# Decayed running sum of a matrix product: two quarters of w trade engines, and the first piece of x is turned and used in two halves

## The chip, the cores and the metric

The kernel runs on one core of a Trainium2 chip. A core has a matrix engine (TensorE, PE in the profile, with its weight loads shown apart as PEld), three engines for element-wise work (VectorE or DVE, ScalarE or ACT, GpSimd or POOL), a queue engine (SyncE or SP) and 16 DMA engines. The metric is the time of one execution on the device in microseconds, lower is better; the median of several runs is given.

## The reference

```python
def setup_inputs():
    B, S, D = (16, 2048, 1024)
    return {'x': np.random.randn(B, S, D).astype(np.float32), 'w': np.random.randn(D, D).astype(np.float32), 'decay': (0.9 * np.random.rand(D) + 0.05).astype(np.float32)}

def reference(x, w, decay):
    xw = x @ w
    out = np.zeros_like(xw)
    out[:, 0, :] = xw[:, 0, :].copy()
    for t in range(1, S):
        out[:, t, :] = decay[None, :] * out[:, t - 1, :] + xw[:, t, :]
    return out.astype(np.float32)
```

A product of x (16 batches of 2048 steps of 1024 values) with one 1024 x 1024 matrix, and then, in each of the 1024 columns, a running sum over the steps that decays by that column's factor.

## The kernel before

**Tiling.** Time is cut into chunks of 512 steps, 64 chunks in all, and pairs of chunks of one batch form groups. The 1024 output columns are eight tiles of 128 (n = 0 to 7), and the contraction over 1024 is eight passes of 128 (k = 0 to 7). Output tiles stand with the columns on the partitions and time along the row, so that the decayed sum is one scan instruction of VectorE along the row. Each pair (group, n) is a slot: eight passes of k for each of its two chunks, 16 matmuls of 512 columns, accumulated in a PSUM tile of two banks ("ps", three of them in a ring; "spare" and "spare1" are one bank each).

**x.** A chunk is loaded by four DMAs from GpSimd's queue, one for each group of 32 partitions (`load`, L105), which turn f32 into bf16 on the way. VectorE transposes it in 32 x 32 blocks on pairs of bf16 values seen as one f32 (`turn`, L115): m names a pair of passes, k = 2m and 2m + 1, and j the block of 32 steps. ScalarE or VectorE then separates even from odd (`part`, L123), which gives "xt". A matmul may take its moving operand from xt, or straight from the transposed pairs "xw" with a stride (the argument `pairs` of `matmul`, L131).

**w.** It is loaded in four quarters (`load_w`, L319): h is the half of the columns, e tells even from odd k. Of each quarter four casts (`settle`, L326), one for each k, bring it into its place in "wsb". Number i of a cast means h = i // 8, e = i // 4 % 2, m = i % 4. So 0 to 3 are the first quarter, 4 to 7 the second, 8 to 11 the third (columns n = 4 to 7, even k) and 12 to 15 the fourth (n = 4 to 7, odd k). The first quarter comes from the queues of SyncE and ScalarE, the other three from GpSimd's.

**Slots after the product.** A paired slot has its odd steps joined with the even steps before them, so that the scan runs over half the length: ScalarE copies the PSUM tile (letter p, L191) and makes the decayed even ones (g, L171), GpSimd adds (j, L205), VectorE scans (S, L210), ScalarE and GpSimd fill in the other half (h and c, L171 and L266). An unpaired slot is scanned by VectorE from PSUM directly (S, L229); slots 1 and 3 are such, slots 0 and 2 are paired. VectorE transposes the result back (B, L278), SyncE stores it (L302). k saves the last value for the next group (L270), z prepares the first (L199, L201), d copies the squared decays (L385).

**Order.** Every instruction is pinned to the order in which it is written; each engine carries out its own in that order. The order is an agenda written out by hand, a list of two- or three-character deeds for each step (a slot number, or -99 for the opening). Capital W settles on VectorE, small w on ScalarE; E is a transpose of one m of one of the four first pieces of x, F and G are the even-odd casts of such a piece on VectorE and ScalarE; M, U and L are loads. The matmuls of slots 0 to 3 are written at step 0, ahead of the deeds of that step; those of slot s at step s.

**The opening.** Chunks 0 and 1 come in two pieces each (`cuts`: ten and six blocks of 32 steps for chunk 0, seven and nine for chunk 1). Ten passes of TensorE on zeros (five f32 matmuls, two passes each, L345) run while the first piece is on its way. `spin_on(3)` (K3) has ScalarE copy one value of the first piece's last 32 partitions into "gate", and one bf16 matmul on gate follows it. Then come the transposes, and the matmuls of slots 0 to 3, first over all eight k of the first piece (even k from xw, odd k from xt), then of the second piece, then of chunk 1. Slot 0 to 2 use the three ps tiles, slot 3 the spares. Slot 4 is the first that reads the third and fourth quarters of w, even k first and then odd k, and its PSUM tile is slot 0's.

Of the kernel before, what the change touches and what calls it, by code (L numbers as in the profile page):

```python
# [14 lines left out]
def _ap(ap_obj: bass.AP, new_ap, extra_offset=0):  # L15
    return dataclasses.replace(
        ap_obj,
        ap=[list(p) for p in new_ap],
        offset=ap_obj.offset + extra_offset,
    )  # L20
# [5 lines left out]
def kernel(  # L26
# [26 lines left out]
    nc = tc.nc  # L53
    pin = tc.keep_in_program_order
    B, S, D = x.shape
# [3 lines left out]
    P = 32  # L59
    CQ = D // NQ  # L60
    K = CQ // P
    M = K // 2
    TL = 512
    NJ = TL // P
    NC = S // TL
    R = K // 2
# [9 lines left out]
    def ring(pool, name, count, shape, dtype=FP32):  # L76
        i = turns[name] = turns.get(name, -1) + 1
        return pool.tile(shape, dtype, name=f"{name}{i % count}")

    def quad(q):  # L80
        return slice(q * P, (q + 1) * P)
# [15 lines left out]
    xb_of = {}  # L97
    xw_of = {}
    xt_of = {}
# [10 lines left out]
    def turn(c, j0=0, j1=NJ, m0=0, m1=M):  # L110
        if c not in xw_of:
            xw_of[c] = ring(sb, "xw", 2, [128, M, NJ, P, 2], BF16)
        src = xb_of[c][:, j0:j1].rearrange("p j c -> p (j c)").bitcast(FP32)
        dst = xw_of[c].rearrange("p m j i e -> p (m j i e)").bitcast(FP32)
        pin(nc.vector.transpose(  # L115
            out=dst.rearrange("p (m j i) -> p j m i", m=M, i=P)[:, j0:j1, m0:m1],
            in_=src.rearrange("p (j m c) -> p j m c", m=M, c=P)[:, :, m0:m1]))
# [7 lines left out]
    def matmul(ps, n, k, xt, t0=0, t1=TL, start=0, pairs=None):  # L125
        if pairs is None:
            rhs = xt[:, k // 2, k % 2, t0:t1]
        else:
            rhs = pairs[:, k // 2, t0 // P:t1 // P, :, k % 2].rearrange("p j i -> p (j i)")
        lhs = wsb[:, k, n].rearrange("p q i -> p (q i)")  # L130
        pin(nc.tensor.matmul(  # L131
            out=ps[:, t0:t1] if ps.shape[1] >= t1 else ps,
            lhsT=lhs,
            rhs=rhs,
            start=(k == 0 and t0 == start),
            stop=(k == K - 1),
        ))
# [192 lines left out]
    idle = wide[:, 0:TL // 2].bitcast(BF16)  # L330
# [9 lines left out]
    gate = const.tile([128, 128], BF16, name="gate")  # L340
    pin(nc.vector.memset(gate, 0.0))

    def spin(count, by, on):
        for _ in range(count):
            pin(nc.tensor.matmul(out=spare, lhsT=by, rhs=on, start=True, stop=True))  # L345

    spin(5, seed, wide)
    H = NJ // 2
    cuts = (((0, H + 2), (H + 2, NJ)), ((0, H - 1), (H - 1, NJ)))
    for q in range(NQ):  # L350
        pin(nc.sync.dma_start(
            out=rows[q * P:q * P + R],
            in_=_ap(decay, [[P, R], [CH, 2], [1, P]], q * CR)))
# [3 lines left out]
        for q in range(NQ):  # L357
            load(i // 2, q, *cuts[i // 2][i % 2])

    def spin_on(q):  # L360
        pin(nc.scalar.copy(out=gate[quad(q), 0:1], in_=xb_of[0][quad(q), 0, 0:1]))  # L361
        spin(1, gate, idle)

    def load_part(i):
        load_w((nc.gpsimd,), *((0, 1), (1, 0), (1, 1))[i])
# [1 line left out]
    def part_one(i, copy):  # L367
        part(i // 8, copy, i % 4, i % 4 + 1, *cuts[i // 8][i // 4 % 2])
# [39 lines left out]
    def finale():  # L408
        six, six_late = ring(psp, "ps", 3, [128, TL]), ring(psp, "ps", 3, [128, TL])
        seven, seven_late = ring(psp, "spare", 1, [128, TL]), ring(psp, "ps", 3, [128, TL])  # L410
        return tuple((early[:, 0:TL // 2], late[:, TL // 2:TL])
                     for early, late in ((six, six_late), (seven, seven_late)))

    def half_of(n, half, ks=range(K)):
        ps = finals[n % R - 2][half]
        t = half * (TL // 2)
        for k in ks:
            matmul(ps, n, k, xt_of[nch - 1], t, t + TL // 2, t)
# [49 lines left out]
    def turn_and_load(c):  # L468
# [19 lines left out]
        "E": lambda i: turn(i // 8, *cuts[i // 8][i // 4 % 2], i % 4, i % 4 + 1),  # L488
        "F": lambda i: part_one(i, nc.vector.tensor_copy),
        "G": lambda i: part_one(i, nc.scalar.copy),  # L490
        "K": spin_on,
        "D": decays,
        "d": square_again,
        "I": identity,
# [14 lines left out]
        "L": lambda i: load(*loads.pop(0)) if loads else None,  # L509
    }  # L510
    agenda = {
        -99: "M0 U0 M1 M2 M3 U1 U2 w0 W1 w2 W3 K3 E0 E1 G0 E2 G1 E3 F2 G3 W4 w5 W6 W7 D E4 E5 G4 E6 G5 E7 F6 G7 E8 E9 G8 E10 G9 E11 F10 G11 E12 L E13 G12 L E14 G13 E15 L F14 G15",
        0: "p0 z0 W8 W9 W10 W11",
        1: "g0",
        2: "L S1 L",
        3: "p2 z2 L w12 w13 w14 w15 g2 j0 S3 L L k1",
        4: "j2 B1 d k3",
        5: "p4 L S0 L g4 S2 L k0 h0 j4 B3 h2",
        6: "k2 c0 T2 c2 p5 g5 B0 L X2 L",
# [58 lines left out]
    def usual(s):  # L578
        paired = [t.paired for t in tiles]
        do = [f"P{s}"] if paired[s] else []  # L580
        if paired[s - 1]:
            do.append(f"S{s - 1}")
        if not paired[s]:
            do.append(f"S{s}")
        do.append(f"C{s - 1}")
        if paired[s - 2]:
            do.append(f"B{s - 2}")
        if not paired[s - 1]:
            do.append(f"B{s - 1}")
        return do + later.get(s, []) + ["L"] * (2 if len(loads) > NQ else 1)  # L590
# [14 lines left out]
    for step, (g, n) in enumerate(slots):  # L605
        T = TL * len(g)
        left = step - len(slots)
        if n % R == 0:
            ns, nj = range(n, n + R), T // P
            if left == -2 * R:  # L610
                outlets = [Outlet(ns, H, half) for half in range(2)]
            else:
                pieces = 1 if left < -7 * R else 2 if left < -6 * R else nj // H
                outlets = [Outlet(ns, nj, pieces=pieces)]
        if left == -R:
            outlets = []
        if step == 0:
            heads = [ring(psp, "ps", 3, [128, T]) for _ in range(3)]
            firsts = [ps[:, 0:TL] for ps in heads] + [spares[0]]
            seconds = [ps[:, TL:T] for ps in heads] + [spares[1]]  # L620
            for j0, j1 in cuts[0]:
                for e in range(2):
                    for k in range(e, K, 2):
                        for i in range(R):
                            matmul(firsts[i], i, k, xt_of[0], j0 * P, j1 * P, j0 * P,
                                   pairs=None if e else xw_of[0])
            Q = cuts[1][0][1] * P
            for k0 in range(0, K, 2):
                for i in range(R):
                    for k in (k0, k0 + 1):  # L630
                        matmul(seconds[i], i, k, xt_of[1], 0, Q,
                               pairs=xw_of[1] if k0 < 4 else None)
            for i in range(R):
                for k in range(K):
                    matmul(seconds[i], i, k, xt_of[1], Q, TL, Q,
                           pairs=xw_of[1] if i < 2 else None)
        if step < R:
            ps = heads[n] if n < 3 else tuple(spares)
        else:
            if step == K + 1:  # L640
                ps = nexts
            elif left >= -2:
                finals = finals if left == -1 else finale()
                ps = finals[left + 2]
            elif len(g) == 2 or n % R < 3:
                ps = ring(psp, "ps", 3, [128, T])
            else:
                ps = ring(psp, "spare", 1, [128, TL])
            todo = [(k, l) for k in range(K) for l in range(len(g))]
            if step < K:  # L650
                todo.sort(key=lambda kl: kl[0] % 2)
            elif step == K:
                todo = []
                nexts = (ring(psp, "spare", 1, [128, TL]), ring(psp, "ps", 3, [128, T])[:, TL:T])
                for l in range(len(g)):
                    for i, one in enumerate((ps[:, l * TL:(l + 1) * TL], nexts[l])):
                        for k in range(K):
                            matmul(one, n + i, k, xt_of.get(g[l]),
                                   pairs=xw_of[g[l]] if l or not i and k >= M else None)
            elif step == K + 1:  # L660
                todo = []
            if left == -2:
                for m, half in ((n, 0), (n + 1, 0), (n, 1)):
                    half_of(m, half)
            if left >= -2:
                todo = []
            if 40 <= step < 180:
                pin(nc.tensor.nop(hint="room", nofuse=True))
            for k, l in todo:
                matmul(ps[:, l * TL:(l + 1) * TL], n, k, xt_of[g[l]])  # L670
        tiles.append(Tile(g, n, ps, outlets))
        do = agenda.get(step, agenda.get(left) if left >= -20 else None)
        if do is None:
            do = usual(step)
        else:
            do = do.split()
            if left == -20:
                do = rest(step) + do
        perform(do)
# [29 lines left out]
```

## Time and profile before

| what | value |
|---|---|
| median of 3 runs | 903.88 us (903.63 to 903.97) |
| profiled execution | 903.37 us |
| its span, first to last instruction | 901.6 us |
| TensorE busy | 894.0 us (99%) |
| VectorE busy | 825.1 us (92%) |
| ScalarE busy | 686.4 us (76%) |
| GpSimd busy | 656.8 us (73%) |
| matmuls of 128 x 512 into ps | 4032 with one other form, mean 377 ns each |
| matmul spacing at 512 columns | 0.216 us |

The durations of matmuls overlap, since the next one starts while the one before drains; the spacing of starts tells what a matmul takes from the end. The profile attributes each wait to what ended it. Idle time of an engine that nobody waits for costs nothing. A line such as "24.90 15.05 PE ... x68" in the timeline is a run of 68 alike instructions from 24.90 us on that lasts 15.05 us.

### The profile page before, as it was taken

Reading aid. Unit: us, or ns where it says so; the run is one execution under the profiler, and the core shown is the slowest. Engines: PE = TensorE matmul, PEld = TensorE weight load, DVE = VectorE, ACT = ScalarE, POOL = GpSimd, SP = SyncE. Lnnn points to the kernel's source line nnn. Section 1 sums busy time; section 2 is a strip of 40 time slices with the busy share of each in tenths; the row PEclk is TensorE's granted clock in tenths of the full one; section 3 lists DMA queues with packets and bytes.
Section 4 is the critical chain, followed back from the end, with each engine's and each line's share of the span. In section 5 each row is a group of like instructions: output and inputs, shape, how many; then the busy total and the mean of one; then the engine's idle time right before and its main releaser. Section 6 shows DMA issues by size and latency. Waiting matters only on the chain.

```text
span 901.6 us, 12277 instructions
## 1 busy us (share of the span) xinstructions
PE 894.0 (99%) x4203; PEld 412.1 (46%) x4203; DVE 825.1 (92%) x631; ACT 686.4 (76%) x958; POOL 656.8 (73%) x756
## 2 busy tenths in 40 slices
PE   8999999999999999999999999999999999999998
PEld 5444444444444444444444444444444444444444
DVE  4999988999999999999998999999999999999998
ACT  4889867777877877877778778777787787787743
POOL 8888678877767768677677677777777776876532
PEclk9999999999999999999999999999999999999999
DMA  9999999999999999999999999999999999999758
GB/s 194 198 215 219 231 235 213 217 225 235 254 252 252 249 236 250 251 249 249 224 237 227 223 233 225 230 229 225 234 228 227 231 235 220 227 228 217 183 142 236
DMA packets 403182, 204.77 MB, mean 227 GB/s; under 512 B 9392, under 2 KB 402096, under 8 KB 403120
## 3 DMA queue, kind: packets, MB, share of 16 engines
q1 hardware_dynamic: 265808, 134.77, 60.4%
q0 software_dynamic: 137024, 68.70, 56.6%
q8 instruction: 33, 0.54, 0.2%
q10 hardware_dynamic: 288, 0.52, 0.2%
q14 instruction: 29, 0.24, 0.1%
HBM read 138.42 MB, written 134.22 MB: 302 GB/s over the span
## 4 chain that ended last, share of the span: by engine, by line
PE 98%; DMA 1%; POOL 0%; issue 0%; DVE 0%; DVEq 0%; ACT 0%; ACTq 0%; POOLq 0%
PE ps L131 97%; PE spare L131 1%; DMA xb<-in_x_dram 1%; POOL xb L105 0%; PE spare L405 0%; PE ps L405 0%; DVE h L426 0%; PE spare L345 0%; DVEq L704 0%; ACT gate L361 0%; ACTq L361 0%; POOLq L693 0%
## 5 line engine op out<-in xcount | busy, mean ns | idle before, releaser
L131 PE MATMUL ps<-xt,wsb 128*128 128x512 bf16 (+1 forms) x4032 | 866.0, 377 | 0.0
L131 PEld LDWEIGHTS <-wsb 128*128 128x128 bf16 x4176 | 407.7, 98 | 477.4 <-ACT wsb L326 1.4
L205 POOL TENSOR_TENSOR xs<-h,xs 128x512 f32<-128x512 f32 (+1 forms) x190 | 242.7, 1278 | 186.7 <-ACT h L171 84.9
L278 DVE STREAM_TRANSPOSE ot<-so 128x1024 f32<-128x1024 f32 (+2 forms) x264 | 300.2, 1175 | 5.0 <-DMA out_dram<-ot 2.6
L191 ACT COPY xs<-ps 128x1024 f32<-128x1024 f32 (+1 forms) x190 | 188.9, 994 | 150.7 <-PE ps L131 145.5
L266 POOL TENSOR_TENSOR so<-h,xs 128x512 f32<-128x512 f32 (+1 forms) x189 | 240.3, 1273 | 43.0 <-ACT h L171 26.0
L123 ACT COPY xt<-xw 128x2048 bf16<-128x2048 bf16 (+4 forms) x136 | 242.3, 1790 | 7.5 <-DVE xw L115 7.4
L105 POOL DMA_DIRECT2D xb<-in_x_dram x264 | 174.1, 661 | 5.2 <-DMA xb<-in_x_dram 2.6
L171 ACT ACTIVATE h<-so,dec 128x512 f32<-128x512 f32 (+1 forms) x189 | 144.9, 767 | 28.9 <-DVE so L210 25.9
L115 DVE STREAM_TRANSPOSE xw<-xb 128x2048 f32<-128x2048 f32 (+4 forms) x78 | 147.3, 1900 | 6.8 <-DMA xb<-in_x_dram 6.8
L210 DVE TENSOR_TENSOR_SCAN so<-spare,keep,xs 128x512 f32<-128x512 f32 (+1 forms) x97 | 119.8, 1237 | 25.5 <-POOL xs L205 25.1
L210 DVE TENSOR_TENSOR_SCAN so<-spare,xs 128x512 f32<-128x512 f32 x93 | 113.2, 1218 | 26.4 <-POOL xs L205 23.6
L171 ACT ACTIVATE h<-ps,dec 128x512 f32<-128x512 f32 (+1 forms) x190 | 129.9, 684 | 0.0
L229 DVE TENSOR_TENSOR_SCAN so<-dec,ps 128x1024 f32<-128x1024 f32 x34 | 76.8, 2260 | 0.8 <-ACT h L171 0.6
L229 DVE TENSOR_TENSOR_SCAN so<-dec,keep,ps 128x1024 f32<-128x1024 f32 (+2 forms) x35 | 75.4, 2153 | 0.0
L270 ACT COPY keep<-so 128x1 f32<-128x1 f32 x136 | 25.4, 189 | 9.2 <-DVE so L229 8.7
L201 ACT COPY so<-keep 128x1 f32<-128x1 f32 x97 | 18.5, 192 | 2.6 <-DVE ot L278 2.4
L131 PE MATMUL spare<-xt,wsb 128*128 128x512 bf16 (+5 forms) x60 | 12.6, 330 | 0.0
L131 PE MATMUL ps<-xw,wsb 128*128 128x512 bf16 (+4 forms) x72 | 12.3, 307 | 0.0
L199 POOL MEMSET so<- 128x1 f32 x93 | 10.6, 116 | 0.6 <-DVE ot L278 0.6
L345 PE MATMUL spare<-wide,seed 128*128 128x512 f32 x10 | 6.8, 842 | 3.2 <-ACT seed L338 3.2
L319 POOL DMA_DIRECT2D ot<-in_w_dram x12 | 6.5, 547 | 0.7 <-DMA xb<-in_x_dram 0.5
(42 smaller groups left out, 37.8 us busy)
## 6 DMA issues: line engine op xcount, KB each, us to landing
out_dram<-ot SPq DMA_DIRECT2D x236, 512.0 KB, 10.8
xb<-in_x_dram POOLq DMA_DIRECT2D x248, 256.0 KB, 7.8
out_dram<-ot SPq DMA_DIRECT2D x56, 128.0 KB, 2.5
out_dram<-ot SPq DMA_DIRECT2D x8, 256.0 KB, 4.1
ot<-in_w_dram POOLq DMA_DIRECT2D x12, 128.0 KB, 6.1
out_dram<-xb SPq DMA_DIRECT2D x3, 256.0 KB
xb<-in_x_dram POOLq DMA_DIRECT2D x4, 160.0 KB, 6.5
xb<-in_x_dram POOLq DMA_DIRECT2D x4, 144.0 KB, 4.5
```

The lines of the kernel that those rows point to most:

```text
L105: pin(nc.gpsimd.dma_start(out=xb_of[c][quad(q), j0:j1], in_=_ap(x, [[D, P], [P * D, j1 - j0], [1, CQ]], (b * S + t0 + j0 * P) * D + q * CQ)))
L115: pin(nc.vector.transpose(out=dst.rearrange("p (m j i) -> p j m i", m=M, i=P)[:, j0:j1, m0:m1], in_=src.rearrange("p (j m c) -> p j m c", ...
L123: pin(copy(out=xt_of[c][:, m0:m1, :, j0 * P:j1 * P], in_=src))
L131: pin(nc.tensor.matmul(out=ps[:, t0:t1] if ps.shape[1] >= t1 else ps, lhsT=lhs, rhs=rhs, start=(k == 0 and t0 == start), stop=(k == K - 1),))
L171: pin(nc.scalar.activation(out=h[:, i * size:(i + 1) * size], in_=src, func=mybir.ActivationFunctionType.Copy, scale=dec[:, self.n:self.n ...
L191: pin(nc.scalar.copy(out=self.xs[:, i * size:(i + 1) * size], in_=ps))
L205: pin(nc.gpsimd.tensor_tensor(out=odds, in0=self.g, in1=odds, op=ALU.add))
L210: pin(nc.vector.tensor_tensor_scan(out=so[:, 3:T + 2:2], data0=squares[-1][:, n:n + 1].to_broadcast([128, T // 2]), data1=self.xs[:, 1:T:2 ...
L229: pin(nc.vector.tensor_tensor_scan(out=so[:, t + 2:t + 2 + size], data0=dec[:, n:n + 1].to_broadcast([128, size]), data1=ps, initial=befor ...
L266: pin(nc.gpsimd.tensor_tensor(out=self.so[:, 2:T + 2:2], in0=self.h, in1=self.xs[:, 0:T:2], op=ALU.add))
L270: pin(nc.scalar.copy(out=self.keep, in_=self.so[:, self.T + 1:self.T + 2]))
L278: pin(nc.vector.transpose(out=outlet.ot[:, :, c0:c0 + P], in_=self.so[:, 2 + t0:2 + t0 + nj * P].rearrange("p (i t) -> p i t", t=P)))
```

## The change

Four things are altered.

1. The gate copy on ScalarE (`spin_on`) is removed. The bf16 matmul on gate stays, but directly behind the five f32 ones, where it waits for nothing of x.
2. The first transpose, ten blocks of m = 0, becomes two of five blocks (`first_turns`, letter e). The four matmuls of k = 0 on that piece become eight: four on the first 160 columns, four on the second. Only the first of each four clears its accumulator (`start`), since the second writes columns of the same bank that were not yet written.
3. Third quarter of w: casts 8 to 11 go from VectorE at step 0 to ScalarE at step 1, behind slot 0's copy and product (p0, g0). Fourth quarter: casts 12 to 15 go from ScalarE to VectorE, at the same place of step 3.
4. Slot 1's scan (S1) is written at step 1, ahead of the w casts; it was between two loads of step 2. On VectorE it so comes before the casts of w, where it came behind those of the third quarter.

```diff
     spin(5, seed, wide)
+    spin(1, gate, idle)
...
-    def spin_on(q):
-        pin(nc.scalar.copy(out=gate[quad(q), 0:1], in_=xb_of[0][quad(q), 0, 0:1]))
-        spin(1, gate, idle)
+    def first_turns(i):
+        J = cuts[0][0][1]
+        turn(0, 0, J // 2, 0, 1)
+        turn(0, J // 2, J, 0, 1)
...
-        "K": spin_on,
+        "e": first_turns,
...
-        -99: "M0 U0 M1 M2 M3 U1 U2 w0 W1 w2 W3 K3 E0 E1 G0 E2 G1 E3 F2 G3 W4 w5 W6 W7 D E4 E5 G4 E6 G5 E7 F6 G7 E8 E9 G8 E10 G9 E11 F10 G11 E12 L E13 G12 L E14 G13 E15 L F14 G15",
-        0: "p0 z0 W8 W9 W10 W11",
-        1: "g0",
-        2: "L S1 L",
-        3: "p2 z2 L w12 w13 w14 w15 g2 j0 S3 L L k1",
+        -99: "M0 U0 M1 M2 M3 U1 U2 w0 W1 w2 W3 e E1 G0 E2 G1 E3 F2 G3 W4 w5 W6 W7 D E4 E5 G4 E6 G5 E7 F6 G7 E8 E9 G8 E10 G9 E11 F10 G11 E12 L E13 G12 L E14 G13 E15 L F14 G15",
+        0: "p0 z0",
+        1: "g0 S1 w8 w9 w10 w11",
+        2: "L L",
+        3: "p2 z2 L W12 W13 W14 W15 g2 j0 S3 L L k1",
...
-            for j0, j1 in cuts[0]:
-                for e in range(2):
-                    for k in range(e, K, 2):
-                        for i in range(R):
-                            matmul(firsts[i], i, k, xt_of[0], j0 * P, j1 * P, j0 * P,
-                                   pairs=None if e else xw_of[0])
+            (_, J), _ = cuts[0]
+            entry = [(0, 0, J // 2), (0, J // 2, J)] + [(k, 0, J) for k in (2, 4, 6, 1, 3, 5, 7)]
+            entry += [(k, J, NJ) for k in (0, 2, 4, 6, 1, 3, 5, 7)]
+            for k, j0, j1 in entry:
+                for i in range(R):
+                    matmul(firsts[i], i, k, xt_of[0], j0 * P, j1 * P, j0 // J * J * P,
+                           pairs=None if k % 2 else xw_of[0])
```

## The prediction

> **What bounds the kernel now.** I read the chain of waits first, then the waits by engine, then the timeline of the first 60 us. The chain, by engine:
>
> ```profile
> PE 98%; DMA 1%; POOL 0%; issue 0%; DVE 0%; DVEq 0%; ACT 0%; ACTq 0%; POOLq 0%
> ```
>
> TensorE sets the end; all other engines can be late without cost until a matmul waits. So the question is where TensorE is still idle. The timeline at the start (start us, length us, then the work; in brackets the idle time before it and what ended it):
>
> ```profile
> 3.22 6.75 PE L345 MATMUL spare<-wide,seed 128*128 128x512 f32 x10 [3.22 <-ACT seed L338]
> ...
> 10.05 0.19 ACT L361 COPY gate<-xb 32x1 bf16<-32x1 bf16 x1 [2.10 <-DMA xb<-in_x_dram]
> 10.09 1.69 DVE L115 STREAM_TRANSPOSE xw<-xb 128x320 f32<-128x320 f32 x4 [2.48 <-DMA xb<-in_x_dram]
> ...
> 10.29 0.39 PE L345 MATMUL spare<-wide,gate 128*128 128x512 bf16 x1 [0.32 <-ACT gate L361]
> ...
> 10.66 0.58 PE L131 MATMUL ps<-xw,wsb 128*128 128x320 bf16 x3
> ...
> 11.08 0.30 PE L131 MATMUL spare<-xw,wsb 128*128 128x320 bf16 x1
> 11.22 0.59 PE L131 MATMUL ps<-xw,wsb 128*128 128x320 bf16 x3
> ```
>
> The first ten blocks of x are there at 10.0; VectorE's four transposes follow, and the first real matmul stands at 10.66. What comes between x's landing and 10.66 is the first place to gain. The other is where w's third and fourth quarters are settled:
>
> ```profile
> 23.03 0.69 ACT L171 ACTIVATE h<-ps,dec 128x512 f32<-128x512 f32 x1
> 23.57 1.04 DVE L326 COPY wsb<-ot 128x512 bf16<-128x512 bf16 x4 [1.84 <-DMA ot<-in_w_dram]
> ...
> 24.12 1.01 ACT L191 COPY xs<-ps 128x1024 f32<-128x1024 f32 x1 [0.39 <-PE ps L131]
> 24.53 2.27 DVE L229 TENSOR_TENSOR_SCAN so<-dec,ps 128x1024 f32<-128x1024 f32 x1
> ...
> 25.89 2.18 ACT L326 COPY wsb<-ot 128x512 bf16<-128x512 bf16 x4 [0.76 <-DMA ot<-in_w_dram]
> ...
> 26.56 0.17 PEld L131 LDWEIGHTS <-wsb 128*128 128x128 bf16 x2 [0.27 <-ACT wsb L326]
> ```
>
> ScalarE makes one k of the fourth quarter in about 0.52 us (2.18 over four, less the tail of the last), TensorE uses one up in two matmuls of 0.216, 0.43 us. So TensorE catches up with ScalarE. Among the waits of the weight loads there is one such place in the whole kernel, and the timelines of TensorE over that stretch and just behind it give the loss:
>
> ```profile
> PEld L131 <- ACT wsb L326: 1.4, 4, 0.4
> ```
> ```profile
> 26.62 2.10 PE L131 MATMUL ps<-xt,wsb 128*128 128x512 bf16 x8
> ```
> ```profile
> 28.12 10.96 PE L131 MATMUL ps<-xt,wsb 128*128 128x512 bf16 x50
> ```
>
> The 1.4 us is idle time of the loader, not of the matmuls. Fifty matmuls without a wait take 10.96, that is 0.216 apart and 0.38 for the last. Eight should take 7 x 0.216 + 0.38 = 1.89; they took 2.10. The stall is 0.2 us. From 28.40 to 880 the table of busy time by stretches has TensorE busy for 31.60 of 31.60 and 820.00 of 820.00 us. So no more than 0.2 us plus what the start gives can be won.
>
> **Part 1, the gate copy and its matmul.** ScalarE's gate copy (0.19) goes, and the bf16 matmul behind it no longer waits for x; it follows the ten warming passes. Those start 0.43 us apart at full clock and the last ends its input at about 9.8, so the matmul (0.22 of issue at 512 columns) is over at about 10.0, before anything of x is ready. It was not what held the first real matmul either: the first transpose ran from 10.09 to 10.60 (it alone, in a narrow window of the timeline), and the matmul came 0.06 later. ScalarE had 0.40 us free before its first cast. Price: nothing, hidden under the transpose.
>
> **Part 2, the first turn in halves.** Four transposes take 1.69 at 320 columns and 1.16 at 192 (the row at 14.41): 0.53 / (4 x 128) = 1.04 ns a column. The starts at 320 are 0.39 apart (0.44 the first). A half of 160 columns is 0.17 shorter: the first half ends at 10.43, the first matmul can start at 10.49 instead of 10.66. But two halves cost one fixed part more, 0.39 - 0.33 = 0.06 us, so every later transpose is 0.06 late: the second one of before ended at 11.00, now at 11.06, and the matmuls of k = 2 can't start before 11.12. Before, they started at 11.22, after four matmuls 0.14 apart. So 0.1 us is the most to be had here, whatever the halves cost.
>
> The eight half matmuls are not in the trace; at 320 columns the spacing is 0.14, at 192 it is 0.085 (15.10 to 15.44 for four). By the line through both, 160 columns take 0.071, eight 0.57, ending at 11.06: gain 0.1. If they go no faster than the 192-column ones, eight take 0.68 and end at 11.17: gain 0.05. If each waits out its own weight load (97 ns mean), 0.78 and 11.27: a loss of 0.05. The nearest row is the one at 192, where loads of 97 ns already go 85 apart, so they overlap; I take 0.1 and keep -0.05 to 0.1.
>
> [...]
>
> What follows has cover. The first cast on ScalarE starts 0.06 later (10.70), the third ends at 12.68, and k = 1 needs the first at 12.81. VectorE's cast and the first weight cast behind it slip 0.06: it ends near 12.77, when k = 1 is due at 12.8, so up to 0.03 may go there. The later pieces of x (14.41, 16.79, 19.83) wait for their DMAs, which don't move, and are used at 15.10, 17.79 and 20.91; 0.1 us earlier still leaves 0.3 us or more at each first use, 0.1 at the last transpose (ends 21.39, used from 21.6).
>
> **Part 3, w's third quarter to ScalarE.** Four casts of 0.52 (0.61 alone) leave VectorE and stand on ScalarE behind the odd product that ends at 23.72; the data landed before 23.57. So k = 0, 2, 4, 6 are done at 24.26, 24.78, 25.30, 25.82, and 0.05 more for the signal. The first matmul of that tile moves from 24.90 to 24.80, so they are due at 24.80, 25.23, 25.66, 26.09. Margins 0.5, 0.4, 0.3, 0.2: covered, but shrinking, since ScalarE is again the slower of the two. Queued behind them is slot 2's copy: 24.12 becomes 25.85, its product 27.97 becomes about 26.8, because the four casts of the fourth quarter are gone from ahead of it. Slot 2's bank is wanted again at about 31.8; free by 27.5.
>
> **Part 4, w's fourth quarter to VectorE, the scan ahead of it.** Slot 1's matmuls end near 23.1, so its scan (2.27) runs from 23.1 to 25.4 where VectorE stood idle for 1.84. The fourth quarter lands at 25.8 (ScalarE's wait ended so). Four casts on VectorE start 0.2 apart and end at 26.2, 26.4, 26.6, 26.9; due at 26.52, 26.95, 27.4, 27.8. The margin starts at 0.3 and grows, so the 0.2 us stall goes. VectorE then takes slot 3's scan at 26.85 instead of 26.72: 0.13 later, with its store, the copy of the squares and the two scans from 30.35 behind it. The first of these that TensorE needs is chunk 2's cast (36.01 to 37.9), read at about 38.9: with TensorE 0.3 earlier and the cast 0.13 later, 0.6 us remain.
>
> No DMA is added or removed, and the issuing queues of SyncE and GpSimd keep their order.
>
> **The sum.** 0.1 + 0.2 = 0.3 us. The profiled execution has a span of 901.6 and a time of 903.37, 1.77 around it: 901.3 + 1.77 = 903.07. The median shown is 0.51 above the profiled one, so 903.6.
>
> **The rivals.** (a) The gain is eaten: TensorE starts earlier but meets VectorE (92% busy) or a later landing of x, so the end stays. For it: VectorE is 0.13 late at slot 3's scan. Against: no matmul row from 28.4 on waits, and the tightest use found has 0.6 us. Time 903.7 to 904.0.
>
> (b) Slower: the weight wait moves from the fourth quarter to the third. Place: ScalarE's four casts between 23.64 and 25.82. It costs nothing until they start at 23.85 (0.2 late), and outweighs the 0.3 won from a start at 24.15, 0.5 late. That needs the third quarter to land 0.6 later than the 23.5 seen, or the copy and product of slot 0 ahead of the casts to slip as much. Casts that start 1 us late lose 0.8 and leave 0.8 - 0.3 = 0.5: 904.4. Against: before, the same landing had its own margin of nearly 1 us (24.6 done, 24.9 due, and faster casts), and three runs within 0.34 us say that landings are steady.
>
> (c) The clock. The passes started 0.85 apart until 7.65 and 0.43 apart from 8.09: full clock came 4.4 us after the first. The bf16 matmul that broke the idle time before x moves to its front; the idle stretch is 10.0 to 10.5 instead of 9.8 to 10.3. Were the clock to fall in it and need 4.4 us again, half that is lost: +2.2 - 0.2, 905.9. Against: both stretches are about as long, and before shows no slow matmul behind its own.
> [...]
>
> (d) The edit does less than it says: the halves are paced by loads, and only part 4's 0.2 less 0.05 remains: 903.7. It lies in the forecast's range.
>
> **How the numbers follow.** Forecast with (d), 903.3 to 903.8: 0.62. (a) 0.2. (b) 0.12. (c) 0.04; a gain from nothing that I can name 0.02. The likeliest case gives 903.6. The range runs from 903.1 (0.3 won and the scatter of 0.2 below the median) to 904.3 (most of (b)), leaving out the tails. About 0.2% (1.8 us) is what a measurement of this kernel can tell from no change. Even x's whole way from landing to the first matmul (0.6) with the stall (0.2) is 0.8 us, so faster beyond it has 0.02; slower only by (c), 0.04; within 0.94.
>
> **What would show it.** Right: the first real matmul at about 10.5 of 160 columns, that of k = 2 at 11.1; no wait of a weight load for ScalarE or VectorE behind 24 us; eight matmuls near 26.5 in 1.89; the scan of slot 1 at 23.1; the first full-width matmul at 24.8 and the one after 64 of them 0.3 earlier than before. Wrong: halves 0.1 apart, a wait for ScalarE's casts at 25 to 26, VectorE still on the fourth quarter when TensorE asks, or a wait behind 36 us that was not there.

## The result, and the profile after

The changed kernel takes 906.36 us (median of 14 runs, 904.65 to 908.66); the kernel before, run beside it, 903.94 (14 runs, 903.22 to 905.16). The ratio is 1.0030, 95% interval 1.0022 to 1.0037: slower by about 2.4 us, where 0.3 us less was forecast. Its profiled execution has a span of 906.1 us against 901.6, and a time of 907.87, one of the longer of its runs.

The opening, from the timeline of the changed kernel:

```profile
9.44 0.38 PE L345 MATMUL spare<-wide,gate 128*128 128x512 bf16 x1
...
10.10 1.75 DVE L115 STREAM_TRANSPOSE xw<-xb 128x160 f32<-128x160 f32 x5 [2.47 <-DMA xb<-in_x_dram]
...
10.50 0.38 PE L131 MATMUL ps<-xw,wsb 128*128 128x160 bf16 x3 [0.68 <-DVE xw L115]
...
10.78 0.37 PE L131 MATMUL ps<-xw,wsb 128*128 128x160 bf16 x3
...
11.12 0.59 PE L131 MATMUL ps<-xw,wsb 128*128 128x320 bf16 x3
...
12.70 0.78 DVE L326 COPY wsb<-ot 128x512 bf16<-128x512 bf16 x3 [0.47 <-DMA ot<-in_w_dram]
...
13.14 0.58 PE L131 MATMUL ps<-xt,wsb 128*128 128x320 bf16 x3 [0.16 <-DVE wsb L326]
```

The halves do what they should: first matmul at 10.50, k = 2 at 11.12 instead of 11.22. In this execution the second quarter of w came later than in the one of before (its casts at 12.70, not 12.34), which cost 0.3 us at 13.14, and a later fourth piece of x cost 0.1 more; the first matmul of 512 columns stands at 25.25, 0.35 behind the one of before. That is not where the 4.5 us went. The timeline behind it:

```profile
26.41 4.24 DVE L326 COPY wsb<-ot 128x512 bf16<-128x512 bf16 x4 [0.63 <-DMA ot<-in_w_dram]
26.44 1.30 POOL L205 TENSOR_TENSOR xs<-h,xs 128x512 f32<-128x512 f32 x1
...
27.68 1.31 POOL L105 DMA_DIRECT2D xb<-in_x_dram  x2
...
27.95 0.55 PEld L131 LDWEIGHTS <-wsb 128*128 128x128 bf16 x4 [1.30 <-DVE wsb L326]
27.95 1.04 PE L131 MATMUL ps<-xt,wsb 128*128 128x512 bf16 x4 [0.81 <-DVE wsb L326]
29.00 1.29 POOL L205 TENSOR_TENSOR xs<-h,xs 128x512 f32<-128x512 f32 x1
...
30.51 13.95 PE L131 MATMUL ps<-xt,wsb 128*128 128x512 bf16 x56 [1.52 <-DVE wsb L326]
```

Four casts that took 1.04 us for the third quarter take 4.24 here. In narrow windows the first lasts 1.49, the second 0.28, the third 2.43, the fourth 0.28. The first starts 0.03 us before GpSimd's add of slot 0 (26.44 to 27.74) and ends 0.16 behind that add's end. The third starts at 28.02, while GpSimd issues a load, and ends at 30.45, 0.16 behind the end of its second add. TensorE waits twice. Starts that should be 0.216 apart are 1.19 and 1.90 apart: 2.66 us lost, where 0.2 was to be won.

The table of busy time by stretches (stretch, busy us of PE, PEld, DVE, ACT, POOL with counts, granted clock, DMA share, GB/s) shows a second loss behind it:

```profile
28.00:30.50 2.50, 0.99 (x4) 0.26 (x4) 2.50 (x3) 0.00 (x0) 2.49 (x4) 1.00 1.45 195
30.80:34.20 3.40, 3.40 (x10) 1.24 (x9) 3.29 (x3) 1.00 (x3) 1.37 (x3) 0.50 1.45 196
34.30:40.00 5.70, 5.70 (x28) 2.57 (x27) 5.70 (x6) 4.14 (x9) 4.45 (x4) 1.00 1.35 181
```

For 3.4 us the granted clock is 0.50, and matmuls start 0.43 apart: 1.7 us. The accounts of the profiled execution close: 0.35 + 2.66 + 1.7, less the 0.2 of the old wait, is 4.5, the difference of the spans. Of the 14 runs, six have a mean clock of 0.997 or 0.998 and take 907.58 to 908.66; the eight at 0.999 or 1.000 take 904.65 to 906.55. A stretch at half clock, 3.4 / 2 / 906, lowers the mean by 0.002, so the drop seems to come in some runs and not in others. In this trace the granted clock is full from 6.93 us, half from 30.82, 0.31 behind the end of the second wait, to 34.23, and full again from there. What decides which runs drop was not tested.

### The profile page after: what moved, and what is told of

Same layout as the page of the kernel before. It is cut to its first block, busy times and chain, and to the rows that moved or that the text cites. A ratio compares the mean times of both kernels' runs of the same rounds, so it can differ in the third digit from the quotient of the medians.

```text
span 906.1 us, 12283 instructions
## 1 busy us (share of the span) xinstructions
PE 895.7 (99%) x4207; PEld 412.7 (46%) x4207; DVE 829.0 (91%) x632; ACT 685.9 (76%) x957; POOL 657.3 (73%) x756
## 4 chain that ended last, share of the span: by engine, by line
PE 96%; DMA 2%; POOL 1%; DVE 1%; issue 0%; DVEq 0%; POOLq 0%
PE ps L131 95%; DMA xb<-in_x_dram 1%; PE spare L131 1%; POOL xb L105 1%; DMA ot<-in_w_dram 1%; DVE wsb L326 0%; PE spare L407 0%; PE ps L407 0%; DVE h L428 0%; POOL ot L319 0%; DVEq L707 0%; DVEq L326 0%; POOLq L696 0%
## 5 line engine op out<-in xcount | busy, mean ns | idle before, releaser
L115 DVE STREAM_TRANSPOSE xw<-xb 128x2048 f32<-128x2048 f32 (+5 forms) x79 | 147.4, 1878 | 7.0 <-DMA xb<-in_x_dram 7.0
L229 DVE TENSOR_TENSOR_SCAN so<-dec,ps 128x1024 f32<-128x1024 f32 x34 | 76.9, 2262 | 1.9 <-PE ps L131 1.2
L229 DVE TENSOR_TENSOR_SCAN so<-dec,keep,ps 128x1024 f32<-128x1024 f32 (+2 forms) x35 | 75.5, 2156 | 0.1
L131 PE MATMUL ps<-xw,wsb 128*128 128x512 bf16 (+5 forms) x75 | 12.5, 301 | 0.7 <-DVE xw L115 0.7
```

Of the source, the lines that this page charges most:

```text
L115: pin(nc.vector.transpose(out=dst.rearrange("p (m j i) -> p j m i", m=M, i=P)[:, j0:j1, m0:m1], in_=src.rearrange("p (j m c) -> p j m c", ...
L131: pin(nc.tensor.matmul(out=ps[:, t0:t1] if ps.shape[1] >= t1 else ps, lhsT=lhs, rhs=rhs, start=(k == 0 and t0 == start), stop=(k == K - 1),))
L229: pin(nc.vector.tensor_tensor_scan(out=so[:, t + 2:t + 2 + size], data0=dec[:, n:n + 1].to_broadcast([128, size]), data1=ps, initial=befor ...
```

## The experiments

Theory: VectorE's fast bf16 copies and GpSimd's adds hold each other up, and the loss lies in the w part alone. In the changed kernel two of the four casts lasted 1.49 and 2.43 us and ended 0.16 behind an add's end; beside loads alone, at 23.57 in the kernel before, a cast took 0.28 to 0.43. What the two engines would have in common is not shown by any run. Rivals: the opening costs (clock, landings); the third quarter on ScalarE costs; the casts wait for data. Each time is set against runs of the kernel before on the same chip at the same time (904.46, 904.04 and 904.28 in the three groups).

**1. The opening alone, and the w part alone.**

```diff
(opening only, from the changed kernel)
-        0: "p0 z0",
-        1: "g0 S1 w8 w9 w10 w11",
-        2: "L L",
-        3: "p2 z2 L W12 W13 W14 W15 g2 j0 S3 L L k1",
+        0: "p0 z0 W8 W9 W10 W11",
+        1: "g0",
+        2: "L S1 L",
+        3: "p2 z2 L w12 w13 w14 w15 g2 j0 S3 L L k1",
(w only: the kernel before with the reverse of these lines)
```

> Opening changed (gate copy out, first turn in halves), the settling of w as in the kernel before. [...] Rival (taking the gate's wait away is what costs, by the clock or by later landings): 904.3 or more, or a stretch at half clock.

> Opening as before, the w part and the scan as changed. [...] Rival (the opening costs): no long cast, 903.7.

Opening only: 903.88, ratio 0.9996 (0.9987 to 1.0005), where the theory had 903.8; k = 2 at 11.1, the old short wait for ScalarE in place, full clock (mean 0.999 in the profiled execution, 1.000 in that of the kernel before). W only: 906.87, ratio 1.0026 (1.0015 to 1.0036), where it had 905 to 908.5 and at least one cast of 1.3 us or more. The loss is in the w part; the opening is not told apart from nothing. The profiled execution of w only was a mild one:

```profile
27.51 1.31 POOL L205 TENSOR_TENSOR xs<-h,xs 128x512 f32<-128x512 f32 x1
27.66 2.06 DVE L326 COPY wsb<-ot 128x512 bf16<-128x512 bf16 x4
```

Its first cast started 0.15 into the add, lasted 1.32 and again ended 0.16 behind the add's end; the other three were through 0.74 us later, and TensorE lost 0.1 us. This execution is longer than the kernel before mostly for later pieces of x: TensorE waited 1.1 us at the gate and 1.0 us for a transposed piece. The other runs of this kernel reach 908.25.

**2. The fourth quarter alone on VectorE.**

```diff
(from the kernel before)
-        3: "p2 z2 L w12 w13 w14 w15 g2 j0 S3 L L k1",
+        3: "p2 z2 L W12 W13 W14 W15 g2 j0 S3 L L k1",
```

> The kernel before with one alteration, the four casts of the fourth quarter on VectorE instead of ScalarE, at their old place behind slot 1's scan. Theory: they start near 26.8 beside slot 0's add, the first ends 0.15 behind that add's end, TensorE waits 0.7 us or more in all (it wants the first at 26.6), 0.5 to 4 us above the kernel before. Rival (the cast's engine doesn't matter, the third quarter or the opening costs): within 0.3 us of the kernel before.

906.25, ratio 1.0021 (1.0012 to 1.0030). This one line is enough for about 2 us:

```profile
26.67 1.29 POOL L205 TENSOR_TENSOR xs<-h,xs 128x512 f32<-128x512 f32 x1
27.47 2.05 DVE L326 COPY wsb<-ot 128x512 bf16<-128x512 bf16 x4
...
27.90 1.33 POOL L105 DMA_DIRECT2D xb<-in_x_dram  x2
...
28.83 5.35 PE L131 MATMUL ps<-xt,wsb 128*128 128x512 bf16 x24 [0.77 <-DVE wsb L326]
```

The first cast lasts 1.31 and ends at 28.78, not 0.15 behind the add's end (27.96) but near the end of the load issued next: the expectation missed that. TensorE's starts were 0.93 late there. Later gaps of 0.2 to 0.3 near 41, 52 and 69 us, 0.7 in all, are not in the kernel before. The trace puts the one near 69 down to a scan of VectorE (L229) that TensorE waits for. A gap like it, 0.18 to 0.30 between 66 and 71 us, stands in the profiles of six other runs, with long casts and without. What the gaps near 41 and 52 wait for stays open.

**3. The fourth quarter back on ScalarE.** First in its place behind slot 2's copy, then ahead of that copy.

```diff
(both on ScalarE)
-        3: "p2 z2 L W12 W13 W14 W15 g2 j0 S3 L L k1",
+        3: "p2 z2 L w12 w13 w14 w15 g2 j0 S3 L L k1",
(ahead of slot 2's copy)
+        3: "z2 L w12 w13 w14 w15 p2 g2 j0 S3 L L k1",
```

> The changed kernel with the fourth quarter back on ScalarE, behind the third, so that no fast cast of VectorE stands beside GpSimd's adds. [...] Rival (early matmuls starve whoever casts): waits of 2 us or more, 906.

> The changed kernel with the fourth quarter back on ScalarE, directly behind the third and ahead of slot 2's copy: opening, third quarter and scan as changed, no fast cast of VectorE beside adds. Theory: short waits of TensorE for ScalarE of 0.2 to 0.4 us in all as in the kernel before, full clock, within 0.3 us of the kernel before. Rival (the third quarter on ScalarE costs by itself): 0.5 us or more above it.

904.95, ratio 1.0010 (1.0001 to 1.0019), and 904.96, ratio 1.0006 (0.9998 to 1.0015). In the first, slot 2's copy on ScalarE (1.01 us) stands between the third and fourth quarter; the fourth so starts 0.9 us later than it could directly behind the third, and TensorE waits 1.0 us in all, more than the 0.3 to 0.6 of the theory, which had 903.9 to 904.4. In the second TensorE's waits for ScalarE come to 0.2 us, as in the kernel before; the median lies 0.7 higher all the same, with an interval that includes no difference. In neither does a wait of 2 us appear. Whether the third quarter on ScalarE costs some tenths stays open.

**4. GpSimd's first add moved behind two loads; then its two adds in the other order as well.**

```diff
(slot 0's add behind the loads)
-        3: "p2 z2 L W12 W13 W14 W15 g2 j0 S3 L L k1",
+        3: "p2 z2 L W12 W13 W14 W15 g2 S3 L L j0 k1",
(slot 2's add first)
+        3: "p2 z2 L W12 W13 W14 W15 g2 S3 L L j2 j0 k1",
-        4: "j2 B1 d k3",
+        4: "B1 d k3",
```

> The changed kernel with GpSimd's first add (slot 0) moved behind the two loads that follow it, so that it starts when VectorE's casts are over. [...] Rival (the casts wait for data or for something else than GpSimd's adds): casts of 1.5 and 2.4 again, 906.

> The changed kernel with GpSimd's order at step 3 as three loads, then slot 2's add, then slot 0's. Slot 2's add waits for ScalarE, so GpSimd stands idle for a moment behind the loads and no add runs beside VectorE's casts. Theory (GpSimd's adds, back to back with its loads, hold the casts): no cast over 1.0 us, TensorE waits 0 to 0.7 us for them, 2 us or more below the run with only slot 0's add moved, within 0.7 us of the kernel before. Rival (the loads alone hold a cast until they and what follows are over, whatever follows): one cast of 1.5 us or more again, 906 or more.

The first is the most telling miss: 907.15, ratio 1.0031 (1.0020 to 1.0042), no better than the change, where the theory had 903.4 to 903.9 if adds alone hold a cast up, and 904 to 905 if load issues do so too. VectorE's and GpSimd's timelines there:

```profile
26.33 4.34 DVE L326 COPY wsb<-ot 128x512 bf16<-128x512 bf16 x4
```
```profile
25.70 1.98 POOL L105 DMA_DIRECT2D xb<-in_x_dram  x3
27.78 2.52 POOL L205 TENSOR_TENSOR xs<-h,xs 128x512 f32<-128x512 f32 x2
30.25 1.30 POOL L105 DMA_DIRECT2D xb<-in_x_dram  x2
```

Two casts pass in 0.27 and 0.29. The third starts at 26.71, beside the second of three load issues, and ends at 30.47, 0.16 behind the second add: it lasts 3.75 us, through two loads and two adds that stand back to back. So this cast was caught beside a load, and did not pass between two instructions of GpSimd. The second version changes only what comes behind the loads: slot 2's add, which needs ScalarE's product of slot 2, comes first, and GpSimd was meant to pause for it. It gives 904.43, ratio 0.9998 (0.9989 to 1.0007), with the casts back at their price (timelines of VectorE, GpSimd and ScalarE):

```profile
27.96 1.03 DVE L326 COPY wsb<-ot 128x512 bf16<-128x512 bf16 x4 [0.90 <-DMA ot<-in_w_dram]
```
```profile
27.33 2.01 POOL L105 DMA_DIRECT2D xb<-in_x_dram  x3
29.43 2.54 POOL L205 TENSOR_TENSOR xs<-h,xs 128x512 f32<-128x512 f32 x2
```
```profile
28.40 0.70 ACT L171 ACTIVATE h<-ps,dec 128x512 f32<-128x512 f32 x1
```

The longest cast is 0.43, TensorE loses less than 0.1 us for them, and the clock stays full (mean 1.000). But the pause is not in this profile: ScalarE's product was done at 29.10, the third load ended at 29.34, and the add began at 29.43, as short behind the load (0.10) as in the first version. The third cast began 0.40 us into the second load and passed at that load's end, with the adds still to come; in the first version it began 0.38 into the second load and did not pass. All 11 runs of the second version (903.66 to 905.31) lie below all 7 of the first (906.19 to 908.46), so the order of the adds matters; by what mechanism it helps is not shown.

**5. Without the two adds.**

```diff
-        3: "p2 z2 L W12 W13 W14 W15 g2 j0 S3 L L k1",
-        4: "j2 B1 d k3",
+        3: "p2 z2 L W12 W13 W14 W15 g2 S3 L L k1",
+        4: "B1 d k3",
```

> The changed kernel without GpSimd's adds of slots 0 and 2 (their odd steps stay unjoined, part of the output differs). [...]

904.06, ratio 0.9999 (0.9990 to 1.0008). Within 0.4 us of the kernel before was expected if the adds are what holds the casts up; if load issues alone are enough, a cast of 0.7 to 1.5 us was to remain.

```profile
25.33 2.12 POOL L105 DMA_DIRECT2D xb<-in_x_dram  x3
...
26.18 1.03 DVE L326 COPY wsb<-ot 128x512 bf16<-128x512 bf16 x4 [0.79 <-DMA ot<-in_w_dram]
```

Beside the last two of three loads, with no add behind them, the four casts take 1.03, the longest 0.43. Without the adds the long casts are gone, and the loss with them; the quarter's data came as before, so that the casts wait for data is out as well.

**6. Other forms of VectorE instruction.** Casts that run across (innermost step not one element), a mix of these with ScalarE, 16 extra casts in the middle of the kernel before, and casts done by a scan.

```diff
(across)
+        pin(nc.vector.tensor_copy(
+            out=wcols[:, 2 * m + e, h].rearrange("p q r i -> p q i r"),
+            in_=src.rearrange("p (q r i) -> p q i r", q=NQ, r=R)))
(mix, v is the form above)
+        3: "z2 L v12 w13 v14 w15 p2 g2 j0 S3 L L k1",
(16 extra, at the end of a step)
+        if 80 <= step < 144 and step % 4 == 0:
+            beside(step < 112)
(by a scan)
+        pin(nc.vector.tensor_tensor_scan(
+            out=wsb[:, 2 * m + e, h * R:(h + 1) * R].rearrange("p r q i -> p (r q i)"),
+            data0=wide[:, 0:1].to_broadcast([128, CH]), data1=src,
+            initial=0.0, op0=ALU.mult, op1=ALU.add))
```

> [...]

> [...] Theory: all four are done in time, no wait of TensorE for casts over 0.1 us, 0.1 to 0.5 us below the kernel before. Rival (VectorE is shut out in any form): a wait of 1 us or more and 1.5 us or more above it.

> The kernel before with 16 casts of 128 x 512 bf16 added on VectorE, into a tile that nothing reads: at every fourth slot from 80 to 108 in the fast form, from 112 to 140 in the slow form, among GpSimd's usual adds and loads (73% busy). Theory: the fast ones last 0.28 to 4 us, several over 1.2 and 1 us or more in the mean; the slow ones all 0.5 to 0.8. [...]

> The changed kernel with VectorE's four casts of the fourth quarter done by its scan instruction with a factor of zero (the columns of these weights come out in another order, so the output differs): 1.1 us each by the rows of 512-column scans. [...] Rival (whatever VectorE reads from the stage tile or writes into w's tile is held up): single scans of 2 us or more.

In all four the theory, that only a fast copy is held up, missed. The across casts were to take 0.6 us, an estimate of the author's that no run had shown, and the run 0.0 to 0.7 us more than the kernel before, by the rival 2 us or more; the scans were to last 1.1 to 1.25 us each whatever GpSimd does. Across, mix and scans came out by the rival's numbers. Across: 911.94, ratio 1.0089 (1.0076 to 1.0103); the mix 906.33, 1.0024 (1.0014 to 1.0034). The across form takes 1.28 us at least, not 0.6, and is no way round: its first cast lasted 3.84 in the one and 2.47 in the other, and it holds GpSimd up in turn. In the across kernel

```profile
31.02 2.11 POOL L205 TENSOR_TENSOR xs<-h,xs 128x512 f32<-128x512 f32 x1
...
33.09 3.77 POOL L105 DMA_DIRECT2D xb<-in_x_dram  x1
```

an add of 1.30 takes 2.11 and a load issue of 0.65 takes 3.77. So here each engine held the other up.

The 16 extra casts: 903.96, ratio 0.9998 (0.9989 to 1.0008). The eight plain casts lasted 0.25 to 0.38, the eight across ones 1.28 to 1.41. The place was badly chosen: at the end of a step a cast follows work that waits for GpSimd's add, so each began in the last 0.25 us of an add or behind it, never in its middle. Four plain casts that began 0.16 to 0.23 before an add's end ended 0.15 behind it, as in the changed kernel. The load issues beside the across ones took 1.5 to 1.6 instead of 0.67.

The scans: 910.21, ratio 1.0069 (1.0055 to 1.0083). VectorE's and GpSimd's timelines, the first line a narrow window:

```profile
27.82 2.44 DVE L332 TENSOR_TENSOR_SCAN wsb<-wide,ot 128x512 bf16<-128x512 f32 x1 [0.56 <-DMA ot<-in_w_dram]
...
30.18 3.75 DVE L332 TENSOR_TENSOR_SCAN wsb<-wide,ot 128x512 bf16<-128x512 f32 x2
```
```profile
27.88 1.29 POOL L205 TENSOR_TENSOR xs<-h,xs 128x512 f32<-128x512 f32 x1
29.11 1.31 POOL L105 DMA_DIRECT2D xb<-in_x_dram  x2
30.43 1.30 POOL L205 TENSOR_TENSOR xs<-h,xs 128x512 f32<-128x512 f32 x1
31.66 1.94 POOL L105 DMA_DIRECT2D xb<-in_x_dram  x3
```

The two scans that meet an add last 2.44 and 2.64; the third and fourth, beside loads alone, 1.19 each. The theory that only copies are held up falls. These scans read both inputs from SBUF. The kernel's own scans take one from PSUM, and slot 3's in the kernel before took 1.19 at 26.72, half a microsecond of it beside an add. Whether the second input in SBUF makes the difference, or the tile read or written, was not separated by a run of its own; the loads let the scans of the same tiles pass.

## Why the prediction was wrong

**The step that failed** is part 4, "Four casts on VectorE start 0.2 apart and end at 26.2, 26.4, 26.6, 26.9". The price is that of the casts of the third quarter at 23.57, beside which GpSimd only issued loads. At the new place, 25.9, the same timeline of the kernel before had slot 0's add on GpSimd and more loads behind it:

```profile
25.92 1.30 POOL L205 TENSOR_TENSOR xs<-h,xs 128x512 f32<-128x512 f32 x1
...
27.15 1.31 POOL L105 DMA_DIRECT2D xb<-in_x_dram  x2
```

In the profiled execution the four took 4.24 us; the 0.2 us to be won became 2.66 lost, and the clock's drop behind it cost 1.7 more. What was queued and due was worked out for VectorE, ScalarE and TensorE, and not what GpSimd did in those microseconds. "VectorE still on the fourth quarter when TensorE asks" stands among the prediction's signs of being wrong, but no rival gave a reason or a price for it. A sign was there: casts of 0.28 beside loads stretched now and then, the last one at 23.57 to 0.43. ScalarE's casts at the same place, beside the same add, had started 0.52 us apart: slower alone, but not held up.

**Part 1** held: gate matmul at 9.44, no loss of clock before x.

**Part 2** held to 0.01 us: 10.50 and 11.12 against 10.49 and 11.12. The halves go 0.07 apart, as the line through the two rows has it, with weight loads of 0.096 each that overlap, and so did not set the pace.

**Part 3** held: ScalarE's four casts ran from 24.14 to 26.31, and TensorE did not wait for them in the changed kernel:

```profile
24.14 2.17 ACT L326 COPY wsb<-ot 128x512 bf16<-128x512 bf16 x4
...
25.25 1.89 PE L131 MATMUL ps<-xt,wsb 128*128 128x512 bf16 x8
```

**The sum** of 0.3 came out in one of its two terms. The opening's 0.1 is shown by the start of k = 2 in two executions (11.12 and 11.14 for 11.22); in the time it is not told apart from nothing. The 0.2 of the stall was not won in the changed kernel. Where it nearly was, in the reordered adds and without the adds, the time did not fall either (904.43 and 904.06 against 904.28 and 904.04), but intervals of 0.9 us to either side can't show 0.3.

**The rivals.** (a), a matmul that meets VectorE, is not in the changed kernel's profile behind 34.4 us; it shows as the gap near 69 us in seven of the other runs, for 0.2 to 0.3. (b) saw weights late at slot 4, on the wrong quarter and engine. (c) named the clock at the wrong place: it fell at 30.8, behind the two waits, and cost 1.7 for 3.4 us, where 2.2 for 4.4 was priced. None of them held the cause, and 4% for slower was far too little. That three runs within 0.34 us show steady landings was wrong as well: 14 runs of the kernel before spread over 1.9 us, and in the profiles TensorE waits for a piece of x for up to 1.5 us (the reordered adds).

No version tried beats the kernel before beyond its interval. The opening alone and the reordered adds beat the changed kernel by 2 to 3 us.

## What to carry to other kernels

When work moves to another engine, take its price from a row where the other engines do what they do at the new place. Here GpSimd made the difference: a fast VectorE cast of 0.28 us next to its adds took up to 3.75, most of a run of back-to-back GpSimd work, and that bill is paid by whoever waits for the cast; a slower engine that is not held up can be the better place, as ScalarE was with its 0.52 a cast beside the same add. If the cast must stay, try another order of GpSimd's work there and measure it: taking slot 2's add ahead of slot 0's, both behind the loads, won the loss back (904.43 against 907.15), though the profile does not show why.

## What had not been expected of the hardware

- A waiting cast was not always served between two GpSimd instructions. It took 3.75 us through two loads and two adds (slot 0's add moved), and 2.43 through two loads and one add (the changed kernel; the first load in each case already under way), yet in several other executions one that met the end of a load passed at the boundary to the next load, or to an add, in 0.43. Nor did the row that starts first win: the changed kernel's first cast begins 0.03 us before the add and ends 0.16 behind it, the second scan begins 0.25 us before its add and ends 1.09 behind it. What decides this stays open.
- Waits of 0.81 and 1.52 us with 1.0 us of work between them were followed by half clock over 3.4 us; one wait of 1.89 us (slot 0's add moved, mean clock 1.000) was not. In the profiled execution of the scans, with waits of 1.69 and 1.95 us, the mean granted clock was 0.996, as in that of the across kernel, against 0.997 in the changed kernel's.
- A VectorE copy of 128 x 512 bf16 that reads with an innermost step of 32 elements and writes with one of 128 took 1.28 us at the least, 4.6 times the plain one's 0.28, and load issues of GpSimd beside it took 1.5 to 1.6 us (16 extra casts) and up to 3.77 (across).
